# Block products of the FFN: weights prepared as quarters, the second block product accumulated onto a copy, and one fixed order

## The chip, the cores and the metric

One core of one Trainium2 chip runs the kernel. The metric is the device time of one execution in microseconds; three runs of the kernel before gave 2365.12, 2362.39 and 2360.70 us, median 2362.39.

## What is computed

Two layers of an encoder over 512 tokens of width 1024. Each layer is a half-step feed-forward network (FFN), a mixer of three branches, and a second FFN, all ahead of a shared adaLN modulation:

```python
D_MODEL, SEQ, DEPTH, D_FF = 1024, 512, 2, 2816
...
def swiglu(h, w_gate, w_up, w_down):
    return (jax.nn.silu(h @ w_gate) * (h @ w_up)) @ w_down
...
    for l in range(DEPTH):
        mod = (c_act @ w_ada[l] + b_ada[l]).reshape(B, N_MOD, D_MODEL)
        h = modulate(rms_norm(x, norm_gain[l, 0]), mod[:, 0], mod[:, 1])
        x = x + 0.5 * mod[:, 2][:, None, :] * swiglu(h, ffn_w_gate[l, 0], ffn_w_up[l, 0], ffn_w_down[l, 0])
        h = modulate(rms_norm(x, norm_gain[l, 1]), mod[:, 3], mod[:, 4])
        x = x + mod[:, 5][:, None, :] * hybrid_mixer(h, ...)
        h = modulate(rms_norm(x, norm_gain[l, 2]), mod[:, 6], mod[:, 7])
        x = x + 0.5 * mod[:, 8][:, None, :] * swiglu(h, ffn_w_gate[l, 1], ffn_w_up[l, 1], ffn_w_down[l, 1])
```

All is float32. The change lies in `h @ w_gate` and `h @ w_up` of the four FFNs.

## The kernel before

**Numbers in two parts.** TensorE (PE) multiplies a rounded type, fp32r. So each operand is split: a high part, which is a cast of the number on ScalarE (ACT), and a low part, which is number minus high part on VectorE (DVE). A product is then three matmuls: high by high, high by low, low by high. `split_to` (L416 to L418) is the cast and the subtraction; `duo` (L69 to L86) gives a tile for both parts: three buffers of tag w, two of tag ptb. In a tile of tag w the parts begin at one of three places, 0, 8 or 16 floats in (WIDE, ENTRY, NARROW). A load of weights lands in a tile of tag raw, of which there are two, or v2, of which there are four (`side_work`, L285, may put one load of the adaLN weights in between).

**The FFN.** `Ffn.run` goes through the 22 chunks of the hidden width (128 rows each) in three parts of 6, 8 and 8 chunks. In each part the gate and up products of its chunks come first and the down products behind them. The activations (silu of gate, times up) wait, split, in tiles of tag b. The down products go through `k_outer` (L421), whose weights come through `wchunk` (L297): load, cast (L310), subtraction (L312).

**Block products.** Most chunks go in pairs through `seven` (L541 to L585). The two chunks of weights are seen as a 2 by 2 block matrix A (A11 and A12 are the two halves of the contraction of the first chunk, A21 and A22 those of the second) and the tokens as a 2 by 2 matrix B. Seven block products in place of eight give the result; they need the sums S1 = A21 + A22, S2 = S1 − A11, S3 = A11 − A21, S4 = A12 − S2 of the weights, T1 to T4 of the tokens (`Blocks`, made once in an FFN), and sums of the products. A block product is `add_product` (L145 to L152): four steps of the contraction, each with the three matmuls of L149, L150 and L151 over 256 tokens, so 12 matmuls. A pair of chunks takes a seven for gate (sums in PSUM of tag acc) and one for up (tag mm). The order of the products is A11·B11 into x, A12·B21 into y, S2·T2 onto x, S1·T1 into w, S3·T3 onto x, S4·B22 onto w, A22·T4 onto x. Since x is used again and again, its states are copied to SBUF by ACT (L572, L576, L578, L580) before the next product adds to it; DVE's sums of blocks, L549, make the parts of the result. DVE makes S1 in L549 (`tens`) and S2 to S4 in L486 (`minus`). Silu is L592, in `apply`; the product with up is in `act` (L624), whose split follows.

There are 35 such pairs of chunks, in eleven stretches: two of 4 pairs in the first FFN, and 1, 4 and 4 in each of the others. A stretch begins after single chunks or after down products and ends in down products.

**What sets the order.** Each engine runs its instructions in the order of its queue. The queue's order is worked out from the program by the framework's scheduler, which may move an instruction ahead of others where its operands allow. Loads are issued by SyncE (SP) when the tile's slot is free. Tasks with due times (`later`, `poll`) put work of the next norm between the products; they lie outside of the stretches' own work.

The stretch in `Ffn.run` (L676 to L686):

```python
                while n < nf:
                    both = [apply(p, AF.Silu)
                            for p in seven([w_gate[l, s, f0 + n + i] for i in range(2)], blocks, acc, place)]
                    place = NARROW
                    ups = seven([w_up[l, s, f0 + n + i] for i in range(2)], blocks, mmt)
                    for i, sg in enumerate(both):
                        acts.append(self.act(n + i, None, ups[i], sg))
                    n += 2
```

Of the kernel before, what the change touches and what calls it, by code (L numbers as in the profile page):

```python
# [15 lines left out]
F32 = mybir.dt.float32  # L16
# [6 lines left out]
P = 128  # L23
# [17 lines left out]
def encoder_kernel(tc, xT, c, w_ada, b_ada, gains, w_gate, w_up, w_down, w_qkv, w_f, w_ubg,  # L41
# [499 lines left out]
    def seven(srcs, blocks, bank, place=NARROW):  # L541

        raws = []
        for src in srcs:
            side_work()
            raw = st([P, KD, P], F32, "raw", NRAW)
            last["dma"] = nc.sync.dma_start(raw, src).ins
            raws.append(raw)
        tens = lambda o, a, b, op: nc.vector.tensor_tensor(o, a, b, op=op)  # L549
        a11, a12, a21, a22 = raws[0][:, :4], raws[0][:, 4:], raws[1][:, :4], raws[1][:, 4:]  # L550
        ah, al = duo((KD, P), "w", place)
        split_to(ah, al, raws[0])
        bh, bl = duo((4, P), "w", NARROW)
        split_to(bh, bl, a22)
        s12, s34 = st([P, 2, 4, P], F32, "v2", 4), st([P, 2, 4, P], F32, "v2", 4)
        tens(s12[:, 0], a21, a22, ALU.add)
        minus(s34[:, 0], a11, a21)
        minus(s12[:, 1], s12[:, 0], a11)
        minus(s34[:, 1], a12, s12[:, 1])
        pair12, pair34 = duo((2, 4, P), "ptb"), duo((2, 4, P), "ptb")  # L560
        split_to(*pair12, s12)
        split_to(*pair34, s34)
        lefts = {"A11": [(ah[:, k], al[:, k]) for k in range(4)],
                 "A12": [(ah[:, 4 + k], al[:, 4 + k]) for k in range(4)],
                 "A22": [(bh[:, k], bl[:, k]) for k in range(4)]}
        for name, pair, i in (("S1", pair12, 0), ("S2", pair12, 1), ("S3", pair34, 0), ("S4", pair34, 1)):
            lefts[name] = [(pair[0][:, i, k], pair[1][:, i, k]) for k in range(4)]
        x, y, w = bank((P, HALF)), bank((P, HALF)), bank((P, HALF))
        c = st([P, 4, HALF], F32, "v2", 4)
        go = lambda o, left, right, start: add_product(o, lefts[left], blocks.operand(right), start)  # L570
        go(x, "A11", "B11", True)
        nc.scalar.copy(c[:, 0], x)  # L572
        go(y, "A12", "B21", True)
        tens(c[:, 0], y, c[:, 0], ALU.add)
        go(x, "S2", "T2", False)
        nc.scalar.copy(c[:, 1], x)  # L576
# [756 lines left out]
```

## Time and profile before

| | us |
|---|---|
| runs before, median of 3 | 2362.39 |
| profiled execution, its own time | 2362.87 |
| its span, first to last instruction | 2361.1 |
| TensorE busy | 2323.9 |
| VectorE busy | 1770.1 |
| ScalarE busy | 1195.8 |
| the eleven stretches of block products, together | 691.1 |

The profile is one execution on the chip. The span is shorter than the execution's own time, which has the start and the end around it. A busy time counts an engine's instructions; a matmul's end is modelled, so a busy PE need not be at its best rate. A row of a group or of the timeline has the line of the kernel, the engine, the operation, output and inputs by their names in the program, and the shape (partitions by elements, type). In brackets behind a row of the timeline stands how long its engine was idle before it, and whose end released it. The granted clock of TensorE was 1.00 throughout.

### The profile page before, as it was taken

How to read it: one execution, taken by the hardware profiler on the slowest of the kernel's cores; microseconds unless marked ns; L12 is line 12 of the kernel's file. 1: busy time of each engine (PE TensorE's matmuls, PEld its weight loads, DVE VectorE, ACT ScalarE, POOL GpSimd, SP SyncE). 2: the span in 40 equal slices, each digit the busy share in tenths (PEclk: the TensorE clock that was granted, in tenths of full speed). 3: DMA queues.
4: the chain of work that ended last, by engine and by line, in shares of the span. 5: the costliest groups of instructions: out<-in, count | busy, mean ns of one | idle time of the engine just before them, and what ended most of it. 6: DMA issues, size and time to landing. Idle time of an engine off the chain costs nothing.

```text
span 2361.1 us, 37435 instructions
## 1 busy us (share of the span) xinstructions
PE 2323.9 (98%) x14322; PEld 2062.1 (87%) x14322; DVE 1770.1 (75%) x3147; ACT 1195.8 (51%) x2097; POOL 327.3 (14%) x433
## 2 busy tenths in 40 slices
PE   7999999999999999999999999999999999999999
PEld 5898998878888898989999989988888888999898
DVE  8887876787686578878678878677866865878583
ACT  5353554677632363535553636456765324646262
POOL 3000011244412110000000000112443212000000
PEclk9999999999999999999999999999999999999999
DMA  8535353333356524353425353533343654143333
GB/s 282 194 108 183 95 168 97 106 99 110 115 190 219 187 72 161 104 192 108 152 63 174 103 187 108 188 107 99 98 121 105 218 208 166 63 143 108 97 101 106
DMA packets 117975, 325.16 MB, mean 138 GB/s; under 512 B 11650, under 2 KB 13826, under 8 KB 117796
## 3 DMA queue, kind: packets, MB, share of 16 engines
q1 hardware_dynamic: 115106, 314.38, 40.4%
q0 software_dynamic: 2688, 8.39, 1.2%
q8 instruction: 112, 1.84, 0.3%
q14 instruction: 67, 0.55, 0.1%
q10 hardware_dynamic: 2, 0.00, 0.0%
HBM read 312.16 MB, written 6.38 MB: 135 GB/s over the span
## 4 chain that ended last, share of the span: by engine, by line
PE 78%; DVE 13%; ACT 4%; issue 3%; DMA 2%; POOL 0%; SPq 0%; ACTq 0%; DVEq 0%; POOLq 0%
PE acc L140 16%; PE acc L142 16%; PE acc L141 16%; PE mm L142 3%; PE mm L149 3%; PE mm L140 3%; PE mm L151 3%; PE mm L141 3%; PE mm L150 3%; PE acc L149 3%; PE acc L150 3%; PE acc L151 3%; DVE w L418 2%; DVE v L486 2%; DVE v L549 1%
## 5 line engine op out<-in xcount | busy, mean ns | idle before, releaser
L312 DVE TENSOR_TENSOR w<-raw,w 128x1024 fp32r<-128x1024 f32 x247 | 311.8, 1266 | 159.4 <-ACT w L310 159.3
L310 ACT CAST w<-raw 128x1024 fp32r<-128x1024 f32 (+1 forms) x255 | 264.5, 1041 | 271.2 <-PE acc L142 191.6
L140 PE MATMUL acc<-b,w 128*128 128x512 f32 (+1 forms) x960 | 359.7, 375 | 0.0
L141 PE MATMUL acc<-b,w 128*128 128x512 f32 (+1 forms) x960 | 356.2, 371 | 0.0
L142 PE MATMUL acc<-b,w 128*128 128x512 f32 (+1 forms) x960 | 356.2, 371 | 0.0
L142 PEld LDWEIGHTS acc<-b,w 128*128 128x128 f32 x960 | 180.5, 188 | 31.7
L140 PEld LDWEIGHTS acc<-b,w 128*128 128x128 f32 x960 | 180.3, 188 | 30.3
L141 PEld LDWEIGHTS acc<-b,w 128*128 128x128 f32 x960 | 180.4, 188 | 29.8
L417 ACT CAST ptb<-v 128x1024 fp32r<-128x1024 f32 x140 | 146.7, 1050 | 103.2 <-DVE v L486 74.6
L140 PE MATMUL acc<-hhi,w 128*128 128x512 f32 x480 | 191.9, 401 | 2.5 <-ACT hhi L749 1.7
L418 DVE TENSOR_TENSOR ptb<-v,ptb 128x1024 fp32r<-128x1024 f32 x140 | 170.6, 1221 | 28.9 <-ACT ptb L417 28.2
L142 PE MATMUL acc<-hhi,w 128*128 128x512 f32 x480 | 189.0, 394 | 1.1 <-DVE w L312 1.0
L141 PE MATMUL acc<-hlo,w 128*128 128x512 f32 x480 | 188.8, 393 | 1.1 <-DVE hlo L752 1.0
L417 ACT CAST w<-raw 128x1024 fp32r<-128x1024 f32 (+1 forms) x140 | 116.6, 833 | 117.1 <-PE acc L142 55.9
L418 DVE TENSOR_TENSOR w<-raw,w 128x1024 fp32r<-128x1024 f32 (+1 forms) x140 | 132.9, 949 | 13.3 <-ACT w L417 13.3
L140 PE MATMUL acc<-w,hhi 128*128 128x512 f32 x336 | 138.7, 414 | 0.9 <-ACT t L851 0.9
L142 PE MATMUL acc<-w,hlo 128*128 128x512 f32 x336 | 131.9, 392 | 0.0
L141 PE MATMUL acc<-w,hhi 128*128 128x512 f32 x336 | 131.6, 392 | 0.0
L227 DVE CUSTOM_DVE_ANT_0 v<-v,b,badac 128x1024 f32<-128x1024 f32 x87 | 115.5, 1339 | 9.0 <-DMA v<-in_w_ada_dram 8.7
L467 DVE SCALAR_TENSOR_TENSOR xv<-acc,badac,xv 128x512 f32<-128x512 f32 (+1 forms) x112 | 77.2, 690 | 55.3 <-PE acc L142 55.3
L149 PE MATMUL acc<-b,ptb 128*128 128x256 f32 x420 | 116.7, 278 | 0.1
L149 PE MATMUL mm<-b,ptb 128*128 128x256 f32 x420 | 116.5, 277 | 0.0
(312 smaller groups left out, 6609.9 us busy)
## 6 DMA issues: line engine op xcount, KB each, us to landing
raw<-in_w_down_dram SPq DMA_DIRECT2D x88, 512.0 KB, 4.2
v<-in_w_ada_dram SPq DMA_DIRECT2D x87, 512.0 KB, 5.3
raw<-in_w_up_dram SPq DMA_DIRECT2D x82, 512.0 KB, 3.6
raw<-in_w_gate_dram SPq DMA_DIRECT2D x79, 512.0 KB, 3.7
b<-in_w_ada_dram SPq DMA_DIRECT2D x57, 512.0 KB, 4.7
raw<-in_w_ubg_dram SPq DMA_DIRECT2D x56, 512.0 KB, 3.6
raw<-in_w_qkv_dram SPq DMA_DIRECT2D x42, 512.0 KB, 3.7
raw<-in_w_branch_dram SPq DMA_DIRECT2D x24, 512.0 KB, 3.7
```

What stands on the lines that cost most here:

```text
L140: mm(o, lh, rh, start=start, stop=False)
L141: mm(o, lh, rl, start=False, stop=False)
L142: mm(o, ll, rh, start=False, stop=stop)
L149: mm(o, lh, rh, start=start and k == 0, stop=False, skip_group_check=True)
L150: mm(o, lh, rl, start=False, stop=False, skip_group_check=True)
L151: mm(o, ll, rh, start=False, stop=k == 3, skip_group_check=True)
L227: dot = nc.vector.tensor_tensor_reduce(out=raw, in0=raw, in1=silc[0], scale=1.0, scalar=badac[:, l, j, d:d + 1], op0=ALU.mult, op1=ALU.add ...
L310: nc.scalar.copy(hi, raw)
L312: lo_eng.tensor_tensor(lo, raw, hi.bitcast(F32), op=ALU.subtract)
L417: nc.scalar.copy(hi, src)
L418: nc.vector.tensor_tensor(lo, src, hi.bitcast(F32), op=ALU.subtract)
L467: nc.vector.scalar_tensor_tensor(x, acc_j, gate, x, op0=ALU.mult, op1=ALU.add)
```

## The change

`seven` becomes a class `Seven` for the weights of one block product set, and a function `stretch` that runs all pairs of a stretch.

- **Loads.** Four loads of 256 KB in place of two of 512 KB: tile u (tag raw) gets A21 and A11, tile v (tag v2) gets A22 and A12. The loads of block n + 2 are written at the start of block n.
- **Sums in place.** S1 overwrites A21 and S2 overwrites A11 in u, once A11 is split. S3 and S4 come from one subtraction of 1024 columns: v minus S2, repeated twice, into a tile of tag pta. (So S3 here is A22 − S2, which is A11 − A21 in the reading above.)
- **Splits.** A11 alone (tag w, 512 columns), then `pair12` (S1 and S2, tag ptb), `second` (A22 and A12, tag w), `pair34` (S3 and S4, tag ptb), each one cast and one subtraction.
- **The second block product.** After A11·B11, ACT copies x to y, PSUM to PSUM, and A12·B21 is added onto y. The sum of the two on DVE goes, and of the copies to SBUF three remain of four. Silu and the product with up now run over four parts of 256 columns for a pair.
- **The order of products** is A11, S1, S2, A12, S3, S4, A22.
- **One fixed order.** Every ACT and every DVE instruction of a stretch is written through `act_` and `vec_`, and each must be issued after the one before it on its engine. Block n + 1 is prepared (sums and splits) during block n, at fixed places between the products, and the activations of block n are made in block n + 1 at fixed places.
- **Place.** The first block's A11 and second lie at ENTRY; before, only A11 and A12 did.

```diff
@@ -538,51 +538,146 @@
             q0, cols = {"T1": (0, FIRST), "T3": (0, SECOND), "T4": (2, FIRST), "T2": (2, SECOND)}[name]
             return [tuple(part[:, k % 2, cols] for part in self.parts[q0 + k // 2]) for k in range(4)]
 
-    def seven(srcs, blocks, bank, place=NARROW):
-
-        raws = []
-        for src in srcs:
-            side_work()
-            raw = st([P, KD, P], F32, "raw", NRAW)
-            last["dma"] = nc.sync.dma_start(raw, src).ins
-            raws.append(raw)
-        tens = lambda o, a, b, op: nc.vector.tensor_tensor(o, a, b, op=op)
-        a11, a12, a21, a22 = raws[0][:, :4], raws[0][:, 4:], raws[1][:, :4], raws[1][:, 4:]
-        ah, al = duo((KD, P), "w", place)
-        split_to(ah, al, raws[0])
-        bh, bl = duo((4, P), "w", NARROW)
-        split_to(bh, bl, a22)
-        s12, s34 = st([P, 2, 4, P], F32, "v2", 4), st([P, 2, 4, P], F32, "v2", 4)
-        tens(s12[:, 0], a21, a22, ALU.add)
-        minus(s34[:, 0], a11, a21)
-        minus(s12[:, 1], s12[:, 0], a11)
-        minus(s34[:, 1], a12, s12[:, 1])
-        pair12, pair34 = duo((2, 4, P), "ptb"), duo((2, 4, P), "ptb")
-        split_to(*pair12, s12)
-        split_to(*pair34, s34)
...
-        x, y, w = bank((P, HALF)), bank((P, HALF)), bank((P, HALF))
-        c = st([P, 4, HALF], F32, "v2", 4)
-        go = lambda o, left, right, start: add_product(o, lefts[left], blocks.operand(right), start)
-        go(x, "A11", "B11", True)
-        nc.scalar.copy(c[:, 0], x)
-        go(y, "A12", "B21", True)
-        tens(c[:, 0], y, c[:, 0], ALU.add)
-        go(x, "S2", "T2", False)
-        nc.scalar.copy(c[:, 1], x)
-        go(w, "S1", "T1", True)
-        nc.scalar.copy(c[:, 2], w)
-        go(x, "S3", "T3", False)
-        nc.scalar.copy(c[:, 3], x)
-        go(w, "S4", "B22", False)
-        tens(c[:, 1], w, c[:, 1], ALU.add)
-        tens(c[:, 3], c[:, 2], c[:, 3], ALU.add)
-        go(x, "A22", "T4", False)
-        return [[c[:, 0:2].rearrange("p a t -> p (a t)")], [x, c[:, 3]]]
+    class Seven:
+
+
+        def __init__(self, srcs, place):
+            top, low = srcs
+            self.place = place
+            self.u = st([P, 2, 4, P], F32, "raw", NRAW)
+            self.v = st([P, 2, 4, P], F32, "v2", 4)
+            for tile_, parts in ((self.u, (low[:, :4], top[:, :4])), (self.v, (low[:, 4:], top[:, 4:]))):
+                side_work()
+                for i, part in enumerate(parts):
+                    last["dma"] = nc.sync.dma_start(tile_[:, i], part).ins
+
+        def put(self, name, pair, src):
+            setattr(self, name, pair)
+            act_(lambda: nc.scalar.copy(pair[0], src))
+            vec_(lambda: nc.vector.tensor_tensor(pair[1], src, pair[0].bitcast(F32), op=ALU.subtract))
+
+        def s1(self):
+            vec_(lambda: nc.vector.tensor_tensor(self.u[:, 0], self.u[:, 0], self.v[:, 0], op=ALU.add))
+
+        def a11(self):
+            self.put("a", duo((4, P), "w", self.place), self.u[:, 1])
+
+        def s234(self):
+            vec_(lambda: nc.vector.tensor_tensor(self.u[:, 1], self.u[:, 0], self.u[:, 1], op=ALU.subtract))
+            self.s34 = st([P, 2, 4, P], F32, "pta", 1)
+            s2 = self.u[:, 1].unsqueeze(1).to_broadcast([P, 2, 4, P])
+            vec_(lambda: nc.vector.tensor_tensor(self.s34, self.v, s2, op=ALU.subtract))
+
+        def pair12(self):
+            self.put("p12", duo((2, 4, P), "ptb"), self.u)
+
+        def second(self):
+            self.put("b", duo((2, 4, P), "w", self.place), self.v)
+
+        def pair34(self):
+            self.put("p34", duo((2, 4, P), "ptb"), self.s34)
+
+        def prepare(self):
+            for step in (self.s1, self.a11, self.s234, self.pair12, self.second, self.pair34):
+                step()
+
...
+    order = {}
+
+    def in_order(engine, fn):
+        if engine in order:
+            with tc.issue_after(order[engine]):
+                order[engine] = fn().ins
+        else:
+            order[engine] = fn().ins
+
+    act_ = lambda fn: in_order("act", fn)
+    vec_ = lambda fn: in_order("vec", fn)
+
+    def stretch(pairs, blocks, acts):
+
+        srcs = [s for pair in pairs for s in pair]
+        order.clear()
+        todo = [Seven(srcs[n], ENTRY if n == 0 else NARROW) for n in range(2)]
+        todo[0].prepare()
+        tens = lambda o, a, b, op: vec_(lambda: nc.vector.tensor_tensor(o, a, b, op=op))
+        snap = lambda o, src: act_(lambda: nc.scalar.copy(o, src))
+
+        def use(up, half, part, silu, product):
+            cols = slice(half * HALF, (half + 1) * HALF)
+            if up:
+                tens(product[:, cols], part, silu[:, cols], ALU.mult)
+            else:
+                act_(lambda: nc.scalar.activation(silu[:, cols], part, AF.Silu))
+
+        def high(pr):
+            a = blk("b")
+            acts.append(a)
+            snap(a[:, 0, :], pr)
+            return a, pr
+
+        def low(a, pr):
+            tens(a[:, 1, :], pr, a[:, 0, :].bitcast(F32), ALU.subtract)
+
+        before = None
+        for n in range(len(srcs)):
+            up = n % 2
+            now = todo.pop(0)
+            nxt = todo[0] if todo else None
+            if n + 2 < len(srcs):
+                todo.append(Seven(srcs[n + 2], NARROW))
+            x, y, w = [(mmt if up else acc)((P, HALF)) for _ in range(3)]
+            c = st([P, 3, HALF], F32, "v2", 4)
+            if not up:
+                silu = [t1(T), t1(T)]
+            product = [t2(T), t2(T)] if up else [None, None]
+            go = lambda o, left, right, start: add_product(o, now.left(left), blocks.operand(right), start)
+            go(x, "A11", "B11", True)
+            split = []
+            if before:
+                use(*before[0])
+                use(*before[1])
+                if not up:
+                    split = [high(before[2][0])]
+            snap(y, x)
+            if split:
+                split.append(high(before[2][1]))
+                for pair in split:
+                    low(*pair)
+            if nxt:
+                nxt.s1()
+                nxt.a11()
+                nxt.s234()
+            go(w, "S1", "T1", True)
+            snap(c[:, 2], w)
+            go(x, "S2", "T2", False)
+            snap(c[:, 0], x)
+            if nxt:
+                nxt.pair12()
+            go(y, "A12", "B21", False)
+            if nxt:
+                nxt.second()
+            go(x, "S3", "T3", False)
+            snap(c[:, 1], x)
+            go(w, "S4", "B22", False)
+            tens(c[:, 1], c[:, 1], c[:, 2], ALU.add)
+            tens(c[:, 0], w, c[:, 0], ALU.add)
+            use(up, 0, y, silu[0], product[0])
+            use(up, 1, c[:, 0], silu[0], product[0])
+            if nxt:
+                nxt.pair34()
+            go(x, "A22", "T4", False)
+            before = (up, 0, x, silu[1], product[1]), (up, 1, c[:, 1], silu[1], product[1]), product
+        use(*before[0])
+        use(*before[1])
+        for pr in product:
+            low(*high(pr))
 
     def apply(parts, func, **kw):
 
@@ -675,15 +770,9 @@
                     n += 1
                 if not opening:
                     blocks.finish()
-                place = ENTRY
-                while n < nf:
-                    both = [apply(p, AF.Silu)
-                            for p in seven([w_gate[l, s, f0 + n + i] for i in range(2)], blocks, acc, place)]
-                    place = NARROW
-                    ups = seven([w_up[l, s, f0 + n + i] for i in range(2)], blocks, mmt)
-                    for i, sg in enumerate(both):
-                        acts.append(self.act(n + i, None, ups[i], sg))
-                    n += 2
+                if n < nf:
+                    stretch([[[w[l, s, f0 + m + i] for i in range(2)] for w in (w_gate, w_up)]
+                             for m in range(n, nf, 2)], blocks, acts)
                 MOD_RATE[0] = 1.2
                 for c0 in (0, T):
                     def src(c):
```

The scheduler's order of the two kernels shows what moves. First ScalarE in the gate seven of the second pair of the first stretch. Names with numbers are single tiles: before, acc_1233 is x, w_1340 the split of A22, ptb_1350 and ptb_1353 those of S1, S2 and of S3, S4, b_1204 an activation of the pair before.

```order
L572 COPY v_214_1236<-acc_1233 128x256
L417 CAST b_1204<-t_197_1201 128x512
L417 CAST w_1340<-raw_1335 128x512
L576 COPY v_214_1236<-acc_1233 128x256
L578 COPY v_214_1236<-acc_1235 128x256
L417 CAST ptb_1350<-v_221_1343 128x1024
L580 COPY v_214_1236<-acc_1233 128x256
L417 CAST ptb_1353<-v_222_1344 128x1024
L592 ACTIVATE t_215_1328<-v_214_1236 128x512
L592 ACTIVATE t_216_1330<-acc_1233 128x256
L592 ACTIVATE t_216_1330<-v_214_1236 128x256
```

The same place of the change; acc_1237 is x, acc_1238 y, acc_1239 w; w_1265 is the split of A11, ptb_1298 that of S1 and S2, w_1314 that of A22 and A12, ptb_1347 that of S3 and S4, all of the next block.

```order
L610 COPY acc_1238<-acc_1237 128x256
L610 CAST b_1260<-t_198_1116 128x512
L556 CAST w_1265<-raw_1105 128x512
L610 COPY v_213_1240<-acc_1239 128x256
L610 COPY v_213_1240<-acc_1237 128x256
L556 CAST ptb_1298<-raw_1105 128x1024
L556 CAST w_1314<-v_192_1106 128x1024
L610 COPY v_213_1240<-acc_1237 128x256
L617 ACTIVATE t_214_1241<-acc_1238 128x256
L617 ACTIVATE t_214_1241<-v_213_1240 128x256
L556 CAST ptb_1347<-pta_1269 128x1024
```

In both, the last copy of x stands behind casts of 1024 columns: one of them, S1 and S2, directly ahead of L580 before, and two, S1 and S2 and the second split, ahead of the last L610 copy now.

VectorE in the same gate seven, before (v_221_1343 holds S1 and S2, v_222_1344 S3 and S4, v_214_1236 the copies):

```order
L624 TENSOR_TENSOR t_197_1201<-mm_1101,t_178_1072 128x256
L418 TENSOR_TENSOR w_1337<-raw_1333,w_1337 128x1024
L418 TENSOR_TENSOR b_1204<-t_197_1201,b_1204 128x512
L549 TENSOR_TENSOR v_214_1236<-acc_1234,v_214_1236 128x256
L418 TENSOR_TENSOR w_1340<-raw_1335,w_1340 128x512
L549 TENSOR_TENSOR v_221_1343<-raw_1335 128x512
L486 TENSOR_TENSOR v_222_1344<-raw_1333,raw_1335 128x512
L486 TENSOR_TENSOR v_221_1343<-v_221_1343,raw_1333 128x512
L486 TENSOR_TENSOR v_222_1344<-raw_1333,v_221_1343 128x512
L418 TENSOR_TENSOR ptb_1350<-v_221_1343,ptb_1350 128x1024
L549 TENSOR_TENSOR v_214_1236<-acc_1235,v_214_1236 128x256
L549 TENSOR_TENSOR v_214_1236<-v_214_1236 128x256
```

And in the change (raw_1105 is u of the next block, v_192_1106 its v, pta_1269 its S3 and S4, v_213_1240 the copies of this one):

```order
L609 TENSOR_TENSOR t_198_1116<-v_196_1114,t_181_992 128x256
L609 TENSOR_TENSOR b_1257<-t_197_1115,b_1257 128x512
L609 TENSOR_TENSOR b_1260<-t_198_1116,b_1260 128x512
L560 TENSOR_TENSOR raw_1105<-raw_1105,v_192_1106 128x512
L557 TENSOR_TENSOR w_1265<-raw_1105,w_1265 128x512
L566 TENSOR_TENSOR raw_1105<-raw_1105 128x512
L569 TENSOR_TENSOR pta_1269<-v_192_1106,raw_1105 128x1024
L557 TENSOR_TENSOR ptb_1298<-raw_1105,ptb_1298 128x1024
L557 TENSOR_TENSOR w_1314<-v_192_1106,w_1314 128x1024
L609 TENSOR_TENSOR v_213_1240<-v_213_1240 128x256
L609 TENSOR_TENSOR v_213_1240<-acc_1239,v_213_1240 128x256
```

Before, VectorE makes the sums and splits within the seven's own time as the scheduler put them; now all sums of the next block stand ahead of its splits, after the last pair's activations and before the sums of this block's products.

Last, ScalarE in the last up seven of the first stretch, where the down products follow (L310 is the cast of a chunk of down weights), before:

```order
L592 ACTIVATE t_292_1846<-acc_1749 128x256
L592 ACTIVATE t_292_1846<-v_290_1752 128x256
L310 CAST w_1989<-raw_1987 128x1024
L572 COPY v_308_1878<-mm_1875 128x256
L310 CAST w_2021<-raw_2019 128x1024
L576 COPY v_308_1878<-mm_1875 128x256
L578 COPY v_308_1878<-mm_1877 128x256
L580 COPY v_308_1878<-mm_1875 128x256
```

And in the change (mm_1873 is x, mm_1874 y):

```order
L617 ACTIVATE t_285_1752<-acc_1747 128x256
L617 ACTIVATE t_285_1752<-v_283_1750 128x256
L310 CAST w_1989<-raw_1987 128x1024
L610 COPY mm_1874<-mm_1873 128x256
L310 CAST w_2021<-raw_2019 128x1024
L610 COPY v_300_1876<-mm_1875 128x256
L610 COPY v_300_1876<-mm_1873 128x256 x2
```

The first chunk's cast stands ahead of the first copy in both; what follows that copy is a copy to SBUF before, and the copy to y now.

More of the change, by code (lines that the diff above doesn't have):

```diff
@@ new lines, in encoder_kernel, with left @@
+    class Seven:
[30 more added lines that the diff above has]
+                step()
+        def left(self, name):
+            if name == "A11":
+                return [(self.a[0][:, k], self.a[1][:, k]) for k in range(4)]
+            pair, i = {"A22": (self.b, 0), "A12": (self.b, 1), "S1": (self.p12, 0), "S2": (self.p12, 1),
+                       "S3": (self.p34, 0), "S4": (self.p34, 1)}[name]
+            return [(pair[0][:, i, k], pair[1][:, i, k]) for k in range(4)]
```

5 lines of the change are left out of this document (removed).

## The prediction

> **What bounds the kernel.** I read the page's sums first, then the busy time of the windows that the change touches, then TensorE's instructions one by one there, then who waits for whom.
>
> ```profile
> PE 2323.9 (98%) x14322; PEld 2062.1 (87%) x14322; DVE 1770.1 (75%) x3147; ACT 1195.8 (51%) x2097; POOL 327.3 (14%) x433
> PE 78%; DVE 13%; ACT 4%; issue 3%; DMA 2%; POOL 0%; SPq 0%; ACTq 0%; DVEq 0%; POOLq 0%
> ```
>
> TensorE (PE) is busy 98% of the span and carries 78% of the chain that ended last; the 13% of VectorE (DVE) and 4% of ScalarE (ACT) on that chain are where PE can gain. The change touches the eleven stretches of block products alone. Their windows (busy time of PE, PEld, DVE, ACT, POOL, then clock, DMA share and GB/s): the first stretch has four pairs, the third only one, and the last row sums all eleven.
>
> ```profile
> 124.60:204.10 79.50, 78.08 (x674) 77.35 (x674) 69.78 (x106) 46.09 (x80) 0.00 (x0) 1.00 0.41 134
> 894.00:913.20 19.20, 19.20 (x170) 19.19 (x169) 15.52 (x24) 9.98 (x18) 0.00 (x0) 1.00 0.60 208
> sum 691.10, PE 680.27 PEld 674.74 DVE 595.90 ACT 399.60 POOL 0.00; mean PE 61.84 PEld 61.34 DVE 54.17 ACT 36.33 POOL 0.00
> ```
>
> 691.10 us for 35 pairs of 14 products. The first matmuls of successive products give the rate of a product (columns: start, duration):
>
> ```profile
> 124.65 0.28 PE L149 MATMUL acc<-hhi,w 128*128 128x256 f32 x1
> 126.07 0.28 PE L149 MATMUL acc<-hhi,w 128*128 128x256 f32 x1
> 127.49 0.28 PE L149 MATMUL acc<-b,ptb 128*128 128x256 f32 x1
> 128.85 0.28 PE L149 MATMUL acc<-b,ptb 128*128 128x256 f32 x1
> ...
> 197.00 0.28 PE L149 MATMUL mm<-b,ptb 128*128 128x256 f32 x1
> 198.42 0.28 PE L149 MATMUL mm<-b,ptb 128*128 128x256 f32 x1
> ```
>
> A product takes 1.36 us (127.49 to 128.85), but 1.42 where a stretch begins (124.65 to 127.49) and here and there after a wait (197.00 to 198.42). The window of one pair, without a wait, is 14 × 1.36 + .16 = 19.20. So the floor is 35 × 14 × 1.36 = 666.4, and the excess is 691.1 − 666.4 = **24.7 us**. The view of waits names its causes (engine and tile that waited, what released it: us in total, times, longest us):
>
> ```profile
> PEld acc L149 <- ACT v L580: 14.3, 22, 0.9
> PE acc L149 <- ACT v L580: 9.7, 18, 0.7
> ACT ptb L417 <- DVE v L486: 74.6, 68, 4.7
> ```
>
> Weight loads and matmuls of L149 wait for the copy in L580, that is A22, the last product of a gate seven, waits until the sum x of S3 has been copied out. The two rows overlap in time, so they aren't added. The third says why the copy is late: the casts of the sums, L417, stand before it on ACT and wait for VectorE's subtractions, L486. One such place, the second pair of the first stretch:
>
> ```profile
> 149.63 0.68 DVE L486 TENSOR_TENSOR v<-raw,raw 128x512 f32<-128x512 f32 x1
> 150.24 0.68 DVE L486 TENSOR_TENSOR v<-v,raw 128x512 f32<-128x512 f32 x1
> 150.96 0.69 DVE L486 TENSOR_TENSOR v<-raw,v 128x512 f32<-128x512 f32 x1
> 151.01 1.05 ACT L417 CAST ptb<-v 128x1024 fp32r<-128x1024 f32 x1 [1.19 <-DVE v L486]
> 151.97 0.36 ACT L580 COPY v<-acc 128x256 f32<-128x256 f32 x1
> 152.09 1.22 DVE L418 TENSOR_TENSOR ptb<-v,ptb 128x1024 fp32r<-128x1024 f32 x1 [0.44 <-ACT ptb L417]
> 152.23 1.05 ACT L417 CAST ptb<-v 128x1024 fp32r<-128x1024 f32 x1
> 152.38 0.39 PE L149 MATMUL acc<-b,w 128*128 128x256 f32 x1 [0.25 <-ACT v L580]
> ```
>
> ACT idled 1.19 us for a subtraction, its cast then held up the copy, and A22's matmul started on the copy's end. The starts of all 490 products divide the 24.7: waits at this place in the 35 gate sevens 13.6 (the row gives 14.3 for the loads alone), other waits 4.5, products at 1.42 some 5, entries 1.6.
>
> **The change, part by part.** For ACT and DVE I take the distance from start to start as an instruction's cost, because a duration overlaps the next:
>
> ```profile
> 146.37 1.21 DVE L418 TENSOR_TENSOR w<-raw,w 128x1024 fp32r<-128x1024 f32 x1
> 147.50 0.68 DVE L418 TENSOR_TENSOR b<-t,b 128x512 fp32r<-128x512 f32 x1
> 148.10 0.41 DVE L549 TENSOR_TENSOR v<-acc,v 128x256 f32<-128x256 f32 x1
> 148.43 0.68 DVE L418 TENSOR_TENSOR w<-raw,w 128x512 fp32r<-128x512 f32 x1
> ...
> 154.49 0.41 ACT L592 ACTIVATE t<-v 128x256 f32<-128x256 f32 x1
> 154.80 1.04 ACT L417 CAST w<-raw 128x1024 fp32r<-128x1024 f32 x1
> 155.74 0.37 ACT L572 COPY v<-mm 128x256 f32<-128x256 f32 x1
> ```
>
> DVE: 1.13 for 1024 columns, .60 for 512, .33 for 256. ACT: .94 for a 1024 cast, .31 for 256 columns, and, an estimate halfway between, .55 for 512.
>
> *Quantity.* DVE, per seven, before: 4 sums of .60, splits of 3 × 1.13 + .60, 3 block sums of .33 = 7.4. After: s1, s2 and A11's split 3 × .60; the joint s34 and three splits 4 × 1.13; 2 block sums of .33 = 7.0. Products with silu and activation splits stay at some 2.5 per pair: 17.2 falls to 16.5 of a pair's 19.04 us. ACT stays near 11. PE's matmuls are the same 168 per pair. So neither helper becomes the bound by quantity; order decides.
>
> *The steady pair.* I walked the new fixed order by these costs, with the handovers of the stall's rows: DVE to ACT .09 (150.24 + .68 to 151.01), ACT to DVE .03 (151.01 + 1.05 to 152.09), ACT to PE .05 (151.97 + .36 to 152.38), t counted from a gate seven's start, products at 0, 1.36, … 8.16. DVE: mults and lows of the last pair until 3.2 (they wait for two short ACT casts); s1, A11's low, s2 until 5.05; s34 6.3; pair12's low 7.4; second's low 8.6; block sums 9.2; pair34's low early in the up seven. ACT: the copy of x to y ends 1.94, A11's cast 2.9, w's copy 3.0, x's after S2 4.66, pair12's cast 5.1 to 6.2, second's cast 7.14, the copy of x after S3 7.4. A22 begins at 8.16 and needs the last: **.76 us of slack where today it is .25 late**. The other two dates: the copy to y must end before S2 writes x (2.72): slack .78; the copy after S2 ends 4.66 against 5.44: the same in size. Nothing waits, so I take the 18 us of waits and the 5 of slow products that follow on them as gone. What is late next: lengthening every handover of the walk by .06 us adds nothing, .10 adds .19 us per pair, .15 adds .49, .20 adds .79.
>
> *PSUM to PSUM copy* (y from x), and A12 accumulating on it. The trace has no such copy, only activations that read PSUM or write it:
>
> ```profile
> L749 ACT ACTIVATE hhi<-t,badac,gainc x8: 812/816/818, 21.2 to 51.2; 128x512 fp32r<-128x512 f32 x8
> L751 ACT ACTIVATE mm<-t,badac,gainc x8: 762/766/766, 21.9 to 51.9; 128x512 f32<-128x512 f32 x8
> ```
>
> Written to SBUF .82 us, written to PSUM .77, each of 512 columns (minimum, median, maximum in ns). So 256 columns into PSUM lie between the .37 of L572 (155.74) and .77. At .77 the copy ends at 2.34, before 2.72. I take .37; both ends add nothing, and in place of a copy and a sum of DVE it saves .33, counted above.
>
> *In place sums and loads.* SP issues the loads of block n+2 when block n's tiles are free: u's after pair12's split, 7.4 us into seven n−1, v's after second's, 8.6. They are read 3.2 us into seven n+1, by the walk more than 12 us later. A quarter load is 256 KB, four for two of 512:
>
> ```profile
> raw<-in_w_gate_dram SPq DMA_DIRECT2D x79, 512.0 KB, 3.7
> strip<-in_rel_dram SPq DMA_DIRECT2D x16, 256.0 KB, 2.7
> 95.00:100.00 5.00, 5.00 (x24) 4.14 (x23) 5.00 (x7) 2.19 (x3) 0.00 (x0) 1.00 0.83 285
> ```
>
> From issue to landing 3.7 us for 512 KB, 2.7 for 256. At 285 GB/s, as this window moved, a quarter occupies the queues for .92 us, four 3.7 of a seven's 9.52. Between 2.7 (beside one another) and 4 × 2.7 = 10.8 (end to end) I take the former, because the window shows overlap: nothing added.
>
> The Trainium skill ("SBUF — State Buffer", § The DMA setup-cost knee) says the contrary of small loads: every transfer pays some 2 us whatever its size, so few large ones are better. By its figures a quarter would be an estimated 2.6 us, four in a row 10.4; the rival on loads below gives the time by rows. The trace's two durations agree with a large fixed part (half the bytes take 2.7 of 3.7 us), but the window shows that it overlaps.
>
> *Entry and exit of a stretch.* At entry A11, S1 are slow as A11, A12 are today, and one more product may read the ENTRY place: 3 × .06 × 11 = 2.0. The exit is the new wait:
>
> ```profile
> 190.66 1.67 SPq L301 DMA_DIRECT2D raw<-in_w_down_dram  x2
> 195.07 1.04 ACT L310 CAST w<-raw 128x1024 fp32r<-128x1024 f32 x1
> 196.01 0.37 ACT L572 COPY v<-mm 128x256 f32<-128x256 f32 x1
> 199.47 1.28 DVE L227 CUSTOM_DVE_ANT_0 v<-v,b,badac 128x1024 f32<-128x1024 f32 x1
> ```
>
> In the last up seven the down chunk's cast stands on ACT ahead of the copy to y, as it stands today ahead of L572's copy. S2, which overwrites x, is the third product in both. Today the copy ends at 196.38, S2 starts at 197.00; in the new order pair34's cast comes first there: until 1.14, two silus until 1.7, the chunk's .94, the copy: 3.0 against 2.72. With handovers .25 to .5; I take **.3 × 11 = 3.3** (.7 each with .06 more per handover; 0 if its cast is passed over). Queued behind the waiting copy on ACT are chunk 1's cast and the remaining copies; nobody on PE needs those for 2.7 us. On DVE the 1.28 of L227, an adaLN product, stands before the last block sums; the activations behind them are needed 6.8 us or more into the down product, which covers it.
>
> *Sum.* 666.4 + 2.0 + 3.3 = 671.7, against 691.1: **−19.4**. The profiled execution took 2362.87 us (span 2361.1, and 1.8 around it); it stands .5 above the median of the runs, so I leave it. 2362.87 − 19.4 = **2343.5**.
>
> **The rivals.** *Part of the waits stays.* In one fixed order an engine can't do what is ready out of turn; if a DVE wait for a load, or handovers of .10 to .15, hit each pair, .2 to .5 us × 35 = 7 to 17 more: 2350 to 2361, most likely below 2358. For it: DVE is busy 87% of a pair, and every item hangs on the other engine. Against: slack of .76.
>
> *The order costs what it saves.* Same chain at .2 us longer handovers: .79 × 35 = 28 in the pairs, some 8 at the exits, 666.4 + 2 + 36 = 704 against 691: **2376**, slower. It decides above .15, where pairs (17) and exits (5) add what today's waits cost. Against: no handover quoted exceeds .1.
>
> *Slow products.* If the new operands (copied y, other pace) kept PE at 1.42: 490 × .06 = 29 − 23 saved, 2369. Against: the pair at 894.00 runs 12 products at 1.36 out of the same tiles, and PE's clock is 1.00 in every window.
>
> *Loads end to end.* 10.8 against 9.52 us, 1.28 for each of 48 sevens (70 less two per stretch) = 61 more: 2405.
>
> *It doesn't do what it says:* the waits move to S2 or to the down chunks, and the total stays: 2358 to 2367.
>
> **How the numbers follow.** Forecast (2339.5 to 2349) .64; part of the waits .20; total unchanged .06; fixed order slower .05, slow products .04, loads .01. The low end is the floor without exit waits and with little entry, 666.4 + 1.2 = 667.6, 23.5 saved; the high end, 2357.5, takes in nine tenths of the second case. 2339.5 to 2357.5 holds .64 + .18 = .82. ±.2% (2357.7 to 2367.1) is about what a measurement of this kernel tells from none: faster .82, same .08 (the unchanged case and the edge of the second), slower .10.
>
> **What would show it.** Right: the windows of four pairs fall from 79.5 to 77 or less; the A22 rows on ACT copies vanish; the copy to y ends .7 before S2; a wait of .3 on it in the last up seven of each stretch. Wrong: a wait row for S2 or A22 of more than .3 us per pair, first products of DVE items waiting for loads, steps of 1.42 in the middle of stretches, a longer gap before the first down product.

## The result and the profile after

The changed kernel takes 2346.12 us in the median of four runs (2344.15 to 2346.59), against 2362.50 before: a ratio of 0.9927 (95% interval 0.9914 to 0.9939), 16.4 us less. The profiled execution took 2346.59 us, with a span of 2344.8 at clock 1.00. First the busy line of its page, then the windows of the stretches (the first, the first one-pair stretch, and the sum of the eleven):

```profile
PE 2315.3 (99%) x14322; PEld 2056.4 (88%) x14322; DVE 1749.1 (75%) x3042; ACT 1194.4 (51%) x2132; POOL 326.1 (14%) x433
```

```profile
124.40:201.50 77.10, 76.88 (x673) 76.69 (x672) 66.34 (x88) 46.89 (x85) 0.00 (x0) 1.00 0.31 107
...
890.80:910.10 19.30, 19.30 (x170) 19.29 (x169) 12.29 (x14) 9.96 (x19) 0.00 (x0) 1.00 0.35 120
...
sum 673.20, PE 671.43 PEld 669.68 DVE 565.41 ACT 405.21 POOL 0.00; mean PE 61.04 PEld 60.88 DVE 51.40 ACT 36.84 POOL 0.00
```

The stretches fell from 691.1 to 673.2 us, 17.9 less; the time between them was 1664.6 against 1662.6 (from matmul starts). The rows of before on A22 and L580 have no successor; in the view of waits all that is left for PE's products in the stretches is:

```profile
PEld mm L149 <- ACT mm L610: 3.3, 8, 0.4
PE mm L149 <- ACT mm L610: 1.8, 8, 0.2
```

That is S2 of the last up seven behind the copy to y, eight times. The place of before's stall, the gate seven of the first stretch's second pair, reads now (ScalarE in the timeline, then PE from A22's first matmul):

```profile
145.22 0.36 ACT L610 COPY acc<-acc 128x256 f32<-128x256 f32 x1 [0.97 <-PE acc L151]
...
148.86 1.05 ACT L556 CAST ptb<-raw 128x1024 fp32r<-128x1024 f32 x1 [0.55 <-DVE raw L566]
149.82 1.04 ACT L556 CAST w<-v 128x1024 fp32r<-128x1024 f32 x1
150.76 0.36 ACT L610 COPY v<-acc 128x256 f32<-128x256 f32 x1
```

```profile
151.48 0.28 PE L149 MATMUL acc<-hhi,ptb 128*128 128x256 f32 x1
151.82 0.28 PE L149 MATMUL acc<-b,w 128*128 128x256 f32 x1
152.16 0.28 PE L149 MATMUL acc<-b,w 128*128 128x256 f32 x1
```

The first cast still waits .55 for S2's subtraction (L566), two casts still stand ahead of the copy, yet the copy ends at 151.12, .70 ahead of A22 at 151.82; PE's steps of .34 run on without a gap.

### The profile page after: what moved, and what is told of

Its sections match the earlier page's. It is cut to its first block, busy times and chain, and to the rows that moved or that the text cites. A ratio compares the mean times of both kernels' runs of the same rounds, so it can differ in the third digit from the quotient of the medians.

```text
span 2344.8 us, 37536 instructions
## 1 busy us (share of the span) xinstructions
PE 2315.3 (99%) x14322; PEld 2056.4 (88%) x14322; DVE 1749.1 (75%) x3042; ACT 1194.4 (51%) x2132; POOL 326.1 (14%) x433
## 4 chain that ended last, share of the span: by engine, by line
PE 50%; DVE 2%; ACT 2%; DMA 1%; issue 0%; POOL 0%; SPq 0%; ACTq 0%; DVEq 0%; POOLq 0%
PE acc L140 9%; PE acc L142 9%; PE acc L141 9%; PE acc L151 3%; PE acc L149 3%; PE acc L150 3%; PE mm L149 3%; PE mm L150 3%; PE mm L151 3%; PE mm L142 2%; PE mm L140 2%; PE mm L141 2%; PE mm L1111 0%; DVE w L312 0%; DMA v<-in_w_ada_dram 0%
## 5 line engine op out<-in xcount | busy, mean ns | idle before, releaser
L310 ACT CAST w<-raw 128x1024 fp32r<-128x1024 f32 (+1 forms) x255 | 264.4, 1041 | 268.1 <-PE acc L142 184.0
L557 DVE TENSOR_TENSOR ptb<-pta,ptb 128x1024 fp32r<-128x1024 f32 x70 | 85.7, 1224 | 50.9 <-ACT ptb L556 49.8
L149 PE MATMUL mm<-b,ptb 128*128 128x256 f32 x420 | 116.9, 278 | 1.8 <-ACT mm L610 1.8
L150 PE MATMUL acc<-b,ptb 128*128 128x256 f32 x420 | 116.1, 276 | 0.0
L151 PE MATMUL acc<-b,ptb 128*128 128x256 f32 x420 | 116.0, 276 | 0.0
L149 PE MATMUL acc<-b,ptb 128*128 128x256 f32 x420 | 116.0, 276 | 0.0
L150 PE MATMUL mm<-b,ptb 128*128 128x256 f32 x420 | 116.0, 276 | 0.0
```

What stands on the lines that cost most here:

```text
L149: mm(o, lh, rh, start=start and k == 0, stop=False, skip_group_check=True)
L150: mm(o, lh, rl, start=False, stop=False, skip_group_check=True)
L151: mm(o, ll, rh, start=False, stop=k == 3, skip_group_check=True)
L310: nc.scalar.copy(hi, raw)
L557: vec_(lambda: nc.vector.tensor_tensor(pair[1], src, pair[0].bitcast(F32), op=ALU.subtract))
```

## The experiments

One profiled run each, unless a count is given; stretches and the rest ("between") from the starts of PE's matmuls, us.

| kernel | time | stretches | between |
|---|---|---|---|
| before | 2362.87 | 691.1 | 1662.6 |
| change | 2346.59 | 673.2 | 1664.6 |
| e1 no fixed order | 2356.03 | 684.2 | 1663.0 |
| e2 sums 1.2 later | 2371.72 | 696.3 | 1666.0 |
| e3 ACT .55 more | 2346.95 | 672.9 | 1665.0 |
| e4 ACT 1.1 more | 2368.68 | 694.1 | 1665.6 |
| e5 no fixed order, PE's held | 2347.41 | 674.0 | 1664.6 |
| e6 down casts after the copy to y | 2340.92 | 668.9 | 1663.2 |
| e7 first block at NARROW | 2365.55 | 691.5 | 1665.1 |
| e8 second block of its own | 2358.81 | 686.3 | 1663.6 |
| e9 the same, its sum early | 2355.80 | 683.2 | 1663.7 |
| e10 e6, A11 alone at ENTRY | 2340.57 (5 runs) | 667.3 | 1663.3 |
| e11 before, sums first | 2347.63 | 677.3 | 1661.2 |
| e12 before, three load tiles | 2359.62 | 685.5 | 1664.8 |

Nine runs of the kernel before, taken beside e9 to e12, lie between 2360.47 and 2365.06, so differences of a few us are read from the stretches and not from the times. In e2 the scheduler also put seven matmuls of the down products into the last up seven of eight stretches; they are counted with the rest.

**How much slack there is (e2, e3, e4).** In each gate seven, needless work lengthens one chain: two subtractions on DVE ahead of S2, or one or two copies on ACT ahead of the copy of x after S3.

```diff
                 nxt.a11()
+                if not up:
+                    for i in range(2):
+                        tens(st([P, 4, P], F32, "ssum", 1), nxt.v[:, 0], nxt.v[:, 1], ALU.subtract)
                 nxt.s234()
...
             go(x, "S3", "T3", False)
+            if not up:
+                for i in range(2):
+                    snap(st([P, 4, P], F32, "ssum", 1), nxt.v[:, i])
             snap(c[:, 1], x)
```

The first addition is e2, the second e4; e3 has one such copy.

> The change with two needless subtractions of 512 columns (1.2 us) on DVE ahead of S2, S3, S4 in each gate seven, 35 in all. Theory (what counts is that the sums are done by 5.3 us, so that the two casts and then the copy of x end .7 ahead of A22): the copy ends 1.2 later, A22 of each gate seven waits .45 to .6, 16 to 21 us in all, and some slow products after it: 16 to 26 us slower than the change. Rival (DVE idles for about 2.5 us of a pair, so 1.2 more is hidden): under 2 us.

> The change with one needless copy of 512 columns (.55 us from start to start) on ACT directly ahead of the copy of x after S3 in each gate seven. In the changed kernel's trace that copy ends .69 ahead of A22. Theory of the walk: hidden, within 1 us of the change. Rival (the fixed order stands at its edge, any lengthening of ACT's chain shows): .2 to .55 for each of 35, 7 to 19 us slower.

> As the one before with two needless copies of 512 columns (1.1 us). Theory of the walk: 1.1 less .69 of slack, .4 for each of 35 gate sevens, 14 us, and up to 7 more for slow products behind the waits: 14 to 21 us slower than the change. If the slack is larger than the trace says: under 5 us. Rival (edge): 1.1 for each, 38 us.

They came out as the walk had it (e4 a little above its range): +25.1, +.4 and +22.1 us against the change's profiled execution. In e3 the copy ended some 8.0 us into the gate seven and A22 began at 8.16. The view of waits of e4:

```profile
PEld acc L149 <- ACT v L610: 11.4, 32, 0.6
PE acc L149 <- ACT v L610: 4.0, 10, 0.4
```

32 of 35 gate sevens wait again at A22, 10.3 us by matmul starts. The stretches grew by 20.9 us; most of the rest is PE going on at 1.41 us a product after a wait, in some 180 products. So a wait of .3 costs about .6 here.

**What holds the gain up (e1, e5).**

```diff
     def in_order(engine, fn):
-        if engine in order:
-            with tc.issue_after(order[engine]):
-                order[engine] = fn().ins
-        else:
-            order[engine] = fn().ins
+        fn()
...
-            mm(o, lh, rh, start=start and k == 0, stop=False, skip_group_check=True)
+            in_order("pe", lambda: mm(o, lh, rh, start=start and k == 0, stop=False, skip_group_check=True))
```

The first piece is e1. e5 adds the second, with the old rule of `in_order` for "pe" alone, on the first and the last matmul of each step; `triple`, of the down products, must come after them too.

> The change without its fixed order: loads, sums, splits, copy to y and order of products stay, but ACT's and DVE's instructions in a stretch lie as the scheduler puts them (the cast of A22 and A12, for one, comes ahead of the copy of w, and the casts of the activations ahead of the copy to y). Theory (the order of ACT and DVE carries the gain): waits of PE on ACT's copies come back, and the stretches, 673.2 us in the change and 691.1 before, take 680 to 691, so the run is 7 to 18 us slower than the change. Rival (the gain is from less DVE work, in place sums and earlier quarter loads, whatever the order): stretches 673 to 675, run within 2 us of the change.

> As the run without the fixed order, but with TensorE's order held as in the change (in the earlier run the first matmul of each next A11 went six products forward and waited there for ACT's cast of A11, so it told nothing of the copies). ACT and DVE lie as the scheduler puts them. Theory (order carries the gain): PE waits for ACT's copies, or DVE's and ACT's splits, at A22, S2 or A11; stretches 676 to 688, against 673.2 in the change and 691.1 before. Rival (less work, earlier loads and in place sums suffice, and the earlier run lost its 11 us by PE's own order alone): 673 to 675.

e1 was 9.4 us slower than the change, in the range of the theory, but not by its mechanism:

```profile
PEld acc L149 <- ACT w L556: 8.2, 14, 0.9
```

PE waited for ACT's cast of A11 (L556), hardly for a copy. The scheduler had also moved the first matmul of each next A11 from the end of the running seven to its second place, six products forward, where A11's split isn't ready. e5 holds TensorE's order alone, and ACT and DVE lie as the scheduler puts them: stretches 674.0, .8 us above the change. The rival holds: **the fixed order of ACT and DVE is worth under 1 us net**. Beside that it keeps the scheduler from moving TensorE's matmuls, which is worth 10.2 us (e1 less e5).

The .8 is a balance. In e5 the last up seven of a stretch no longer waits: its copy to y ends 1.92 to 1.97 us into the seven, where the change has 3.05 in eight stretches. That wait costs the change 4.3 us (e6 below). In turn e5 waits inside the pairs, mostly for the copy to y of a gate seven:

```profile
PEld acc L149 <- ACT acc L610: 1.9, 5, 0.8
```

With the slow products behind such waits e5's stretches take 5.1 us more than those of e6, which has the fixed order and no wait at the exit. So the fixed order saves about 5 us in the pairs and gives 4.3 back at the exits.

**Which part brings it: order of the sums, or earlier loads (e11, e12).** Both start from the kernel before. e11 moves four lines in `seven`, e12 gives the loads a third tile.

```diff
+        s12, s34 = st([P, 2, 4, P], F32, "v2", 4), st([P, 2, 4, P], F32, "v2", 4)
+        tens(s12[:, 0], a21, a22, ALU.add)
+        minus(s34[:, 0], a11, a21)
+        minus(s12[:, 1], s12[:, 0], a11)
+        minus(s34[:, 1], a12, s12[:, 1])
         ah, al = duo((KD, P), "w", place)
         split_to(ah, al, raws[0])
         bh, bl = duo((4, P), "w", NARROW)
         split_to(bh, bl, a22)
-        s12, s34 = ...
...
+            slot[0] += 1
-            raw = st([P, KD, P], F32, "raw", NRAW)
+            raw = st([P, KD, P], F32, *(("pta", 1) if slot[0] % 3 == 0 else ("raw", NRAW)))
```

> The kernel before with one thing moved: in seven the four sums of the weights stand ahead of the splits of A11, A12 and A22. Loads, tiles, order of products and TensorE's order stay. Theory O (before, DVE's order makes the sums late: they stand behind two splits): the waits of A22 on ACT's copy, 13.6 us over the gate sevens, fall under 5, and the stretches from 691.1 to 674 to 684. Theory L (the sums are late because DVE idles for the gate loads, 60.6 us over 35 pairs, and then lags): within 3 us of 691, waits of 10 or more.

> The kernel before with one thing changed: the chunks of the block products go through three tiles in turn (the two of tag raw and the one of tag pta, idle there) in place of two, so each load can start about half a seven, 4.8 us, earlier. The order on ACT, DVE and PE in the steady pairs stays. Theory L (late loads): DVE's waits for gate loads fall from 60.6 us to under 15, the waits of A22 from 13.6 to under 4, stretches from 691.1 to 674 to 682. Theory O (order): waits for loads fall as well, but A22's waits stay at 10 to 14, stretches 687 to 692.

The sums alone bring 13.8 us where the change brings 17.9, the third tile alone 5.5. In both, PE's matmuls in the stretches keep the order of before. The views of waits, e11 first:

```profile
DVE v L549 <- DMA raw<-in_w_gate_dram: 65.0, 35, 4.7
...
PEld mm L149 <- ACT v L572: 5.4, 12, 1.0
```

```profile
DVE v L549 <- DMA raw<-in_w_gate_dram: 29.7, 13, 4.5
DVE v L486 <- DMA raw<-in_w_gate_dram: 18.7, 4, 5.1
DVE v L549 <- DMA pta<-in_w_gate_dram: 5.2, 5, 1.1
PEld acc L149 <- ACT v L580: 11.8, 23, 0.9
```

In e11 DVE waits for gate loads as long as before (65.0 us; 60.6 before), and no A22 waits; what waits is S2 behind the copy after A11 (L572), mostly in up sevens. In e12 A22 still waits in 23 gate sevens (11.0 us by matmul starts, 13.6 before). But e12 did not do what it was built for: DVE's waits for gate loads fall only from 60.6 to 53.6 us (the three DVE rows together), and its 685.5 lies between the two forecasts. So it doesn't price loads that come in time. e11 decides for theory O: the sums were late because DVE made them behind two splits, and with the long waits for loads all in place the waits of A22 are gone.

**Copy to y or a sum of its own (e8, e9).**

```diff
-            c = st([P, 3, HALF], F32, "v2", 4)
+            c = st([P, 4, HALF], F32, "v2", 4)
...
-            snap(y, x)
+            snap(c[:, 3], x)
...
-            go(y, "A12", "B21", False)
+            go(y, "A12", "B21", True)
...
             tens(c[:, 0], w, c[:, 0], ALU.add)
-            use(up, 0, y, silu[0], product[0])
+            tens(c[:, 3], y, c[:, 3], ALU.add)
+            use(up, 0, c[:, 3], silu[0], product[0])
```

That is e8. In e9 the sum into c[:, 3] stands on the line of A12's product instead:

```diff
-            go(y, "A12", "B21", True)
+            go(y, "A12", "B21", True); tens(c[:, 3], y, c[:, 3], ALU.add)
```

> The change with the second block product in PSUM of its own again: x after A11 is copied to SBUF, not to y, A12 starts y, and DVE adds the two (one sum of 256 columns more per seven, .33 us). Order of products and of all else as in the change. Theory (the accumulation onto a copy is worth nothing by itself, since DVE has the .33 free behind the block sums): stretches within 1 us of 673.2. Rival (it carries part of the gain): 35 times .3 to .6 in the gate sevens, 10 to 20 us more.

> As the run with the second block product of its own (686.3 us of stretches, 12.7 us slower than the change), but DVE's sum of the two blocks stands right behind A12, ahead of the second split's low part and not behind the other block sums, so that silu of that part needn't wait for the seven's last sums. Theory (the accumulation onto a copy saves .33 of DVE; what cost 13 us was that silu moved behind the last sums, which pushes the next copy of x after A11 past S2): stretches 673 to 677, most of the loss gone. Rival (the sum itself, in the chain at any place, is the cost): 683 to 687 as before.

I had expected under 1 us and measured 13.1 (stretches), with the sum moved forward still 10.0, so in both the rival came true. Both times S2 of the up seven waits for the copy after A11 (e8):

```profile
PEld mm L149 <- ACT v L610: 11.5, 23, 0.6
PE mm L149 <- ACT v L610: 6.9, 23, 0.4
```

In e9 that copy ends 1.99, 2.51, 2.90 and 3.68 us (the last a mean; in six of the eight stretches 3.80 or more, behind the down cast) into the up sevens of a stretch's four pairs, where S2 is due at 2.72; in the change 1.92, 2.11, 2.11, and 3.05 only in the last, behind the down cast. The delay grows by .4 to .5 from pair to pair until PE waits: with .33 more per seven on DVE, one round through DVE and ACT takes longer than PE's 19.04 us.

**Exit and entry (e6, e7, e10).**

```diff
-            snap(y, x)
+            snap(y, x); gate.update({} if nxt else {"scalar": order["act"]})
...
-        todo = [Seven(srcs[n], ENTRY if n == 0 else NARROW) for n in range(2)]
+        todo = [Seven(srcs[n], NARROW) for n in range(2)]
...
-            self.put("b", duo((2, 4, P), "w", self.place), self.v)
+            self.put("b", duo((2, 4, P), "w", NARROW), self.v)
```

The first is e6, the second e7, the first and third e10. `gate["scalar"]` names the instruction behind which the casts of the down chunks (L310) must be issued.

> The change with one rule more: the casts of the down chunks come behind the copy to y of a stretch's last up seven. In the changed kernel's trace S2 waits .38 there in eight of the eleven stretches, and one of them goes on in slow products. Theory (the cast ahead of that copy is the whole wait): stretches 673.2 less 3.0 to 3.4, 669.8 to 670.2, and nothing given back in the down products. Rival (the down chunk is then late): the same or more time between the stretches, total unchanged.

> The change with the first block's A11, A22 and A12 at the place of all others (NARROW) and not at ENTRY. In the changed kernel's trace the products A11, A12 and A22 of each first seven take 1.41 to 1.42 us, the rest 1.36; 19.27 us for the first pair, 19.04 for the next. Theory A (the place in the tile sets the rate of a product): first pairs 19.04 to 19.1, stretches 2 to 2.5 us less. Theory B (ENTRY is what lets PE fall into its fast step behind the products before): first pairs run slow throughout, up to 19.8, 5 to 6 us more. If neither matters: first pairs unchanged.

> The change with the casts of the down chunks behind the copy to y of the last up seven (668.9 us of stretches in its earlier run), and with only A11 of the first block at ENTRY, A22 and A12 at NARROW as in all other blocks. Theory: A11 at ENTRY is enough for PE's fast step, two slow products per stretch go, .055 each: stretches 667.5 to 668, the run 2339 to 2341.5, 5 to 6 us below the change. Rival: A12 at NARROW brings the slow step back for the first pairs, 672 to 686. No PE wait on ACT's copies in the stretches by either.

The exit in the change (first stretch, timeline), from the last silu on:

```profile
192.68 0.41 ACT L617 ACTIVATE t<-v 128x256 f32<-128x256 f32 x1
...
192.99 1.04 ACT L310 CAST w<-raw 128x1024 fp32r<-128x1024 f32 x1
...
193.93 0.37 ACT L610 COPY mm<-mm 128x256 f32<-128x256 f32 x1
...
194.36 0.38 PE L149 MATMUL mm<-b,ptb 128*128 128x256 f32 x1 [0.22 <-ACT mm L610]
```

The cast of the down chunk (L310) stands between silu and the copy to y, and S2 starts on that copy's end. In e6 the copy comes at once, the wait is gone in all stretches, 4.3 us fall away (3.0 to 3.4 were expected), and nothing is given back between them. e7 gives theory B, and more than its 5 to 6 us: not the first pairs alone, but nearly all products at 1.41 us, 18.3 us more. In the stretches PE's matmuls have the order of the change; only the place of these weights differs. e10, with A11 alone at ENTRY, keeps the fast step and saves two slow products per stretch:

```profile
124.40:200.70 76.30, 76.30 (x674) 76.28 (x673) 68.04 (x93) 46.92 (x85) 0.00 (x0) 1.00 0.35 118
...
sum 667.10, PE 667.10 PEld 666.95 DVE 582.25 ACT 405.18 POOL 0.00; mean PE 60.65 PEld 60.63 DVE 52.93 ACT 36.83 POOL 0.00
```

PE is busy throughout the stretches. e10 has a median of 2340.57 us (2339.40 to 2343.01), a ratio to before of 0.9910 (0.9897 to 0.9924), and beats the change by 5.5 us between medians of different runs, and by 6.1 in the windows.

## Why the prediction was right, and where its steps failed

Forecast were 19.4 us less than the profiled execution of before, 2343.5; its counterpart after shows 16.3 less, 2346.59. Of the 3.1 between them 1.5 lie in the stretches, nearly all of the rest between them.

**The bound, right.** The gain came from where the excess was read: waits of PE on ACT's copies in the stretches. 17.9 us of 24.7 are gone, and e10 leaves .9 above the floor of 666.4.

**The steady pair, right in size.** The walk let the copy to y end 1.94 us into the gate seven, the copy after S2 4.66, the last copy 7.40; the trace has 1.92, 4.65 and 7.47. In up sevens the copy to y ends at 2.11, the walk had the same place as in gate sevens. Slack at A22 was forecast as .76 and is .69, which e3 and e4 bracket: .55 hides, 1.1 shows. e2 shows the cause of the slack, sums that are done early: made 1.2 us later, they bring the waits of A22 back.

**"Order decides", right, but it was not the fixed order.** The walk took the written order as what makes the slack. e11 shows that the sums' place ahead of the splits carries 13.8 us even in the old kernel, and e5 that the chain on ACT and DVE is worth .8 net, some 5 saved in the pairs and 4.3 lost at the exits. The rival "the order costs what it saves" was tied to that chain and so was priced on the wrong thing.

**Exit, mis-sized.** .3 in each of eleven stretches, 3.3, became .5 in seven (.38 of wait, .13 in the step of the product behind it), .75 in the first, where PE went on slowly after the wait, and nothing in the three one-pair stretches, where the copy ended at 2.39: 4.3 in all. **Entry, mis-sized:** 2.0 became 2.5. I had counted A11, S1 and one more as slow; slow are A11, A12 and A22 (1.42 to 1.43), the three that lie at ENTRY, and S1 is partly so (1.38). That the count of three fits is luck. Both terms make 673.2 of the forecast 671.7.

**Outside, taken as nothing.** There the profiled execution lost 2.0 us against that of before. In the runs above this part lies between 1661.2 and 1666.0, and the two kernels built from before span 3.6 of that; the part between a layer's two FFNs' stretches, which holds the mixer, takes 567.4 to 569.2 us (layer 1) and 567.7 to 571.7 (layer 2) outside of e2. So I count it as variation from run to run. That was not tested by repeating one kernel's profile.

**The copy to y, right in cost, wrong in worth.** The copy takes .36, as the low bound had it. But I wrote that it saves .33 of DVE per seven and that neither helper is the bound by quantity; e8 and e9 show that this .33 was worth 10 to 13 us in this order. The busy share that I gave for DVE, 87% of a pair, was no proof of room. As I read it, DVE's instructions wait for ACT's and ACT's for them, and the round is the sum of both; no run tests that by itself.

**The rivals.** Slow products did not come, yet they were nearer than the pair at 894.00, which I held against them, made them look: e7 is that case, 2365.55 against the 2369 that I gave. Its cause is not the one that I named (the copied y, another pace) but the place of the first block's weights. Loads end to end did not show either. The page's rows for quarters of gate weights in the change:

```profile
v<-in_w_gate_dram SPq DMA_DIRECT2D x70, 256.0 KB, 3.7
raw<-in_w_gate_dram SPq DMA_DIRECT2D x70, 256.0 KB, 3.1
```

A quarter takes 3.1 or 3.7 us from issue to landing, where 512 KB took 3.7 before. Yet DVE waits for gate loads at S1 (L560) three times in all, each time ahead of a stretch's first block. The Trainium skill ("SBUF — State Buffer", § The DMA setup-cost knee) is borne out in that half the bytes take nearly as long or as long. Its rule to load in large pieces was not tested here; the small loads hold nothing up, because they are issued early: for S1 at 174.63 us, in the first stretch, the last quarters are issued at 160.06, 14.6 us ahead.

## What to carry to other kernels

Where one helper's queue holds both the work that others wait for and work that nobody waits for yet, put the first ahead; here four lines did most of what a rewrite did. A busy share says little about slack between two engines that feed one another: walk one round by start-to-start times, and test it by adding known work at the place with the least slack. When an order is fixed by hand, look at what the scheduler does to the other engines' queues as well, and at the last round of a loop, where foreign work comes into the queue.

## What the runs showed of the hardware that was not expected

A product of the same twelve matmuls takes 1.36 or 1.41 us at a granted clock of 1.00, and whichever step PE is in lasts for many products. With the first block's weights 16 floats into their tile (e7) the second pair's first matmuls are still .353 apart; with A11 8 floats in they are .34 apart from the third product on. The rows are those of e7:

```profile
144.08 0.28 PE L149 MATMUL acc<-hhi,w 128*128 128x256 f32 x1
144.43 0.28 PE L149 MATMUL acc<-hhi,w 128*128 128x256 f32 x1
144.78 0.28 PE L149 MATMUL acc<-hhi,w 128*128 128x256 f32 x1
```

In e7 nearly all 490 products run so, 18.3 us more, and PE counts as busy all the while, by the sum of its windows:

```profile
sum 691.70, PE 691.70 PEld 691.49 DVE 568.57 ACT 409.39 POOL 0.00; mean PE 62.88 PEld 62.86 DVE 51.69 ACT 37.22 POOL 0.00
```

Only in the last up seven of four of the eleven stretches do they become fast. Products that read the ENTRY place are slow themselves (1.42 to 1.43 in the change), those that follow at other places are fast (1.36). Why a place 32 bytes off sets the step of what comes after is open; no run here tells it.
